# Separate PSUM banks for attention's value products, and one branch's gate blocks placed between the heads' projections

## The chip, the cores and the metric

The kernel runs on one core of a Trainium2 chip. A core has five engines with a queue each: TensorE (PE, matmuls; PEld is its weight load), VectorE (DVE), ScalarE (ACT), GpSimd (POOL) and SyncE (SP, which here issues the weights' transfers). Matmul results go to PSUM, which has eight banks of 128 partitions x 512 float32; VectorE and ScalarE read them from there. The metric is the device time of one execution in microseconds (us); lower is better. Times are the median of several runs, and one more execution is profiled.

## The reference

One layer of a streaming encoder on 512 tokens of width 1024. The change concerns the first sub-layer, four parallel mixers (A to D) that read the same normalized input `h`, and touches the PSUM banks of all later stages.

```python
h = _rms_norm(x, norm_mix_pre[l])
(a_q, a_k, a_v, f_q, f_k, f_v, f_g, c_u, s_x, s_b, s_c) = jnp.split(h @ w_in[l], cuts, axis=-1)
# A: differential attention, 4 heads, chunk-causal: a = softmax(s0) - lam * softmax(s1);  ya = rms_norm(a @ v)
# B: forgetting attention, 8 heads, frame-causal, bias from cumulative log forget gates;  yf = softmax(s + bias) @ v
# C: convolution branch: GLU, causal depthwise conv of width 31, LayerNorm, silu -> yc
# D: short gated convolution: s_b * conv3(s_c * s_x) -> ys
br = jnp.stack([ya, yf, yc, ys], axis=2)
proj = jnp.einsum('bsnc,ncd->bsnd', br, w_branch[l])
gates = jax.nn.sigmoid(h @ w_gate[l] + b_gate[l]).reshape(B, S, N_BRANCH, D)
mixed = jnp.sum(gates * proj, axis=2) @ w_out[l]
x = x + _rms_norm(mixed, norm_mix_post[l])
```

Cross-attention into 256 memory tokens and a gated MLP of width 2816 follow.

## The kernel before

**Arithmetic.** Each float32 operand is split into a high and a low part, and a product is three matmuls (`mm3`, line 185): high x high, high x low, low x high, all issued in line 178. A projection of 128 output channels over 1024 inputs is 8 x 3 = 24 matmuls of 512 columns (`channel_major`, line 191). Transposes are matmuls with an identity (line 182).

**Blocks.** `run_blocks` (line 151) takes jobs from one list, `all_jobs` (line 1268). Most jobs carry a weight block of 512 KB: `load_raw` (line 118) has SP transfer it into `wr` (2 buffers), ACT makes the high part `wh` (line 138) and DVE the low part `wl` (line 139), four buffers each; then the job's body issues its matmuls and the work that reads its PSUM bank. A job that is only a function (`then`, line 894) runs between the bodies.

**Background tasks.** The attention heads, the convolution and the norms are generators in a queue (`Background`, line 44). `bg.tick()` lets up to two of them take steps beside the blocks, by a clock of matmul time and by a cost that each step gives; `bg.drain(name)` runs the tasks of that name to their end.

**Final order.** What is traced is not yet the order on the engines: the framework orders instructions by a timeline of its own, which takes buffers into account, and writes the waits between engines. Each engine then works through its queue in that order.

**PSUM.** `bank(tag)` (line 90) takes one of the eight banks: tag `mm` has four, `sc` (scores) two, `tr` (transposes) two. Before, projections and attention's value products (`values`, line 634) both take `mm`. A value product of a head in A (`a_task`, line 650) takes its bank at step 3 and gives it back after step 5; a task of B (`f_task`, line 793) takes two banks so.

**The order of the mixer** (`mixer_jobs`, line 901): the convolution's input (C), the short convolution (D), D's gates and products, the values of A, then for each of A's four heads its q and k projection (`qk_jobs`, line 591), after which that head's task joins the queue. Then, after `bg.drain("conv")`, the gates of C (`gate_blocks(2, "c")`, line 862): for each of four pairs of output blocks two gate blocks (24 matmuls each, evicted by ACT's tanh in line 871) and one branch block (two products of 12 matmuls, evicted by DVE in line 883 and added in line 884). Then the tasks of A are drained, and the values, q and k of B follow, with A's gates between them.

**A head of A.** `qk_jobs` writes q and k into a tile `qk` (2 buffers; POOL clears two halves of it in line 600) with ACT (lines 604, 612, 613) and DVE (lines 605 and 614, two of each). `a_task` goes through four blocks of 128 queries: scores into two `sc` banks, mask and maximum (DVE, line 671), exponentials (ACT, line 676), the reciprocal and lambda (lines 678, 679), the difference of the two softmaxes (lines 680, 681), a transpose through a `tr` bank, and its split into high and low parts (lines 109, 110), which the value products read. The last steps normalize the head's output (lines 686 to 705).

**Other stages named below.** The bias of B's scores is made on POOL (line 830) and added with the maximum on DVE (line 836). D's B product is read in line 564. The first four up-projections (`up_jobs`, line 1188) are done in two halves of tokens and hold their banks meanwhile; the down-projection (line 1225) uses all eight banks.

Of the kernel before, what the change touches and what calls it, by code (L numbers as in the profile page):

```python
# [16 lines left out]
F32 = mybir.dt.float32  # L17
# [7 lines left out]
P = 128  # L25
# [55 lines left out]
def hybrid_layer(ctx: ExitStack, tc: tile.TileContext, a: dict, out: bass.AP):  # L81
# [5 lines left out]
    psum = ctx.enter_context(tc.tile_pool(name="ps", bufs=4, space=PSUM))  # L87
    dram = ctx.enter_context(tc.tile_pool(name="dr", bufs=1, space=DRAM))

    def bank(tag="mm"):  # L90
        return psum.tile([P, 512], F32, tag=tag, name=f"ps_{tag}", bufs=4 if tag == "mm" else 2)

    x_d, mem_d = a["x"][0], a["mem"][0]
    w_in, w_gate, w_out = a["w_in"][0], a["w_gate"][0], a["w_out"][0]
# [54 lines left out]
    bg = Background(0.7, 2)  # L149
# [140 lines left out]
    for i, plan in enumerate(plans):  # L290
        r_t = m1p.tile([P, P], F32, tag="fbias" if i == 2 else "ck", name=f"rows{i}", bufs=2)
        n = 0
# [10 lines left out]
    for i in range(2):  # L303
        keep(PE.matmul(gain[i], ones, gain_row[:, i * 512:(i + 1) * 512], start=True, stop=True))

    glu = [bank() for _ in range(2)]

    def busy(n):

# [24 lines left out]
    turned = {}  # L334
# [3 lines left out]
        keep(V.scalar_tensor_tensor(y01[t][:, sl], xs[:, t, sl], r01[t], gain[half], ALU.mult, ALU.mult))  # L338

    def turn(t, half):  # L340
        ps = turned[t, half] = bank("mm" if half else "tr")
        for k in range(4):
            keep(PE.transpose(ps[:, k * P:(k + 1) * P], y01[t][:, (half * 4 + k) * P:(half * 4 + k + 1) * P], ident))  # L343

# [43 lines left out]
    w_g = [split_weights(*raw, V, lambda ins: casts.append(keep(ins))) for raw in raw_g]  # L388


    glu.extend(bank() for _ in range(2))
    for i in range(2):
        for p in range(3):
            first_half(i, p, w_g[i], glu[2:])
# [22 lines left out]
    half = {}  # L417
# [232 lines left out]
    def a_task(h, qk, v):  # L650
        es, pt, av = {}, None, None
        for step in range(6):
            if step in (3, 5):
                if av is None:
                    av = bank()
                vh, vl = (x[:, :, h * P:(h + 1) * P] for x in v[0])
                values(av, lambda kt: ((vh[:, kt], 0), (vh[:, kt], 1), (vl[:, kt], 0)), pt, step // 2 - 1)
            cost = 0.0
            if 1 <= step <= 4:
                if step in (1, 3):  # L660
                    pt = pt_tiles()
                to_keys_major(es.pop(step - 1)[:, 0], step, pt[0], pt[1], (step - 1) % 2)
                cost += 0.1 + 0.15 * step
            if step < 4:
                qt, w = step, (step + 1) * P
                e = es[qt] = e4()
                st = m1p.tile([P, 8], F32, tag="st8", name="st8", bufs=4)
                for c in range(2):
                    ps = bank("sc")
                    scores(ps, qk, c, qt * P, w)  # L670
                    V.tensor_tensor_reduce(e[:, c, :w], ps[:, :w], mask_a[:, S - w:], scale=1.0,  # L671
                                           scalar=-3.0e38, op0=ALU.add, op1=ALU.max,
                                           accum_out=st[:, c:c + 1])
                V.tensor_scalar(st[:, 2:4], st[:, 0:2], -HD ** -0.5, None, ALU.mult)
                for c in range(2):
                    A.activation(e[:, c, :w], e[:, c, :w], AF.Exp, bias=st[:, 2 + c:3 + c],
                                 scale=HD ** -0.5, accum_out=st[:, 4 + c:5 + c])
                V.reciprocal(st[:, 6:8], st[:, 4:6])
                V.tensor_scalar(st[:, 7:8], st[:, 7:8], lam, None, ALU.mult)
                A.activation(e[:, 1, :w], e[:, 1, :w], AF.Copy, scale=st[:, 7:8])  # L680
                V.scalar_tensor_tensor(e[:, 0, :w], e[:, 0, :w], st[:, 6:7], e[:, 1, :w], ALU.mult,
                                       ALU.subtract)
                cost += 0.6 + 0.0035 * w
            if step == 5:
                e = e4()
                A.copy(e[:, 0], av)
            yield cost, 3.5

        ps = bank("tr")
        for t in range(NT):  # L690
            transpose(ps[:, t * P:(t + 1) * P], e[:, 0, t * P:(t + 1) * P])
        A.activation(e[:, 1], ps, AF.Square, scale=1.0 / math.sqrt(P))
        ms = m1p.tile([P, NT], F32, tag="ms4", name="ms4", bufs=2)
        V.tensor_reduce(ms, e[:, 1].rearrange("p (t c) -> p t c", t=NT), AX.X, ALU.add)
        r = rstd_of(m1p, [ms], NT)
        V.tensor_tensor(e[:, 0].rearrange("p (t c) -> p t c", t=NT),
                        ps.rearrange("p (t c) -> p t c", t=NT),
                        r.unsqueeze(2).to_broadcast([P, NT, P]), ALU.mult)
        yield 1.5, 3.5
        ps2 = bank("tr")  # L700
        for t in range(NT):
            transpose(ps2[:, t * P:(t + 1) * P], e[:, 0, t * P:(t + 1) * P])
        if "a" not in y:
            y["a"] = (y8(), y8())
        split(ps2, y["a"][0][:, h], y["a"][1][:, h], half["dn"])
        yield 0.6, 0.0
# [5 lines left out]
    def vf_jobs(dst):  # L712

        ps, held = {}, []
        groups = ((0, 256), (256, 520))

        def products(kb, tokens):
            hi, lo = held[kb]
            for t in tokens:
                sl = slice(t * P, (t + 1) * P)  # L720
                for k in range(2):
                    kk = kb * 2 + k
                    for g, (c0, c1) in enumerate(groups):
                        mm3(ps[t, g][:, :c1 - c0], ht[0][:, kk, sl], ht[1][:, kk, sl], hi[:, k, c0:c1],
                            lo[:, k, c0:c1], kk == 0, kk == NK - 1)

        def done(t):
            for g in range(2):
                hs = slice(4 * g, 4 * g + 4)
                split(ps[t, g][:, :256].rearrange("p (h c) -> p h c", h=4), dst[0][:, t, hs, 0], dst[0][:, t, hs, 1])  # L730
            V.tensor_copy(dst[1][:, t], ps[t, 1][:, 256:264])

        for kb in range(4):
            def body(hi, lo, kb=kb):
                held.append((hi, lo))
                if kb == 0:
                    dst.append(m1p.tile([P, NT, 8, 2, HD], F32R, tag="v", name="v"))
                    dst.append(m1p.tile([P, NT, 8], F32, name="fz_raw"))
                    ps.update({(t, g): bank() for t in range(2) for g in range(2)})
                products(kb, (0, 1))  # L740
                if kb < 3:
                    return
                done(0)
                done(1)
                bg.tick()
                ps.update({(t, g): bank() for t in range(2, 4) for g in range(2)})
                for b in range(4):
                    products(b, (2, 3))
                    bg.tick()
                done(2)  # L750
                done(3)
                forget_gates(dst[1])

            yield *cols(w_in, O_FV, BR + 8, kb * 2, 2), body
# [38 lines left out]
    def f_task(p, qk, v):  # L793
# [4 lines left out]
        for j in range(2):  # L798
            t = m1p.tile([P, S], F32, tag="ck", name="ck", bufs=2)
# [3 lines left out]
        es, pts, av = {}, None, None  # L803
        for step in range(6):
            if step in (3, 5):
                if av is None:
                    av = [bank(), bank()]
                for j in range(2):
                    hl = v[0][:, :, 2 * p + j]
                    values(av[j], lambda kt: ((hl[:, kt], 0), (hl[:, kt], 1)), pts[j], step // 2 - 1)  # L810
# [11 lines left out]
            if step < 4:  # L822
# [3 lines left out]
                for j in range(2):  # L826
# [7 lines left out]
                    ps = bank("sc")  # L834
# [59 lines left out]
    def then(f):  # L894

        return None, None, f
# [4 lines left out]
    def mixer_jobs():  # L901
        yield from c_jobs()
        yield then(lambda: bg.add(lam_task(), "lam"))
        yield from d_jobs()
        yield then(lambda: bg.add(conv_norm_task(), "conv"))
        yield from gate_blocks(3, "d")
        yield then(lambda: y.pop("d"))
        yield from v_jobs(O_AV, va)
        for h in range(4):
            yield from qk_jobs(O_AQ, O_AK, h, lambda qk, h=h: bg.add(a_task(h, qk, va), "a"))  # L910
        yield then(lambda: bg.drain("conv"))
        yield from gate_blocks(2, "c")
        yield then(lambda: bg.drain("a"))
        yield from vf_jobs(vf)
        yield from kv_blocks(0)
        ga = gate_blocks(0, "a")
        for p in range(1, 4):
            yield from kv_blocks(p)
            for _ in range(4):
                yield next(ga)  # L920
        yield then(lambda: bg.drain("f"))


    ns = SimpleNamespace()
# [263 lines left out]
    def up_jobs():  # L1188
# [16 lines left out]
        for n in range(2 * NF):  # L1205
            def body(hi, lo, n=n):
                j, i = divmod(n, 2)
                if n > 3:
                    ps = bank()
# [2 lines left out]
                    return  # L1212
                if n == 0:
                    bg.drain("n0")
                ps = bank("mm" if n % 2 else "sc")
                channel_major(ps, (hi, lo), ns.hf, slice(0, S // 2))
                held.append((j, i, ps, (hi, lo)))
                if n == 3:
# [6 lines left out]
    def down_jobs():  # L1225
        tail = 4
        held, ps = [], []
# [5 lines left out]
        for kk in range(NF):  # L1233
            def body(hi, lo, kk=kk):
                if kk == 0:
                    tags = (("mm", "mm"), ("mm", "mm"), ("sc", "sc"), ("tr", "tr"))
                    ps.extend([bank(n) for n in pair] for pair in tags)
                if kk < NF - tail:
                    for t in range(NT):
# [6 lines left out]
                for t in range(NT):  # L1246
# [11 lines left out]
                    for i in range(2):  # L1258
                        sl = slice(i * 512, (i + 1) * 512)
                        parts = 2 if (t, i) == (NT - 1, 1) else 1  # L1260
                        for q in range(parts):
                            n = 512 // parts
# [50 lines left out]
```

## Time and profile before

| | |
|---|---|
| median of 3 runs | 1109.14 us (1108.85 to 1110.48) |
| profiled execution | 1108.61 us, of which its span (first to last instruction) 1106.8 us |
| granted clock of TensorE, mean | 0.998 |
| matmul and weight-load records | 5445 each |
| DMA issues on SP | 207, most of them weight blocks of 512 KB |
| weight cast, ACT line 138 | 180 x 1.05 us |
| weight split, DVE line 139 | 180 x 1.23 us |
| projection matmul, 512 columns, line 178 | record of 0.38 to 0.40 us |
| q eviction, DVE line 605; k eviction, DVE line 614 | 16 x 0.69 us each |
| gate eviction, ACT line 871 | 0.69 us |
| branch eviction, DVE line 883; sum, line 884 | 24 x 0.69 us each |

The stages by time: C's and D's input to about 127 us, D's gates to 195, A's values to 219, A's q and k to 277, C's gates to 363, B's values to 386, B's q and k with A's gates to 524, B's gates to 597, output projection to 640, cross-attention to 731, the MLP to the end.

How the profile is read: a share of busy time is an average over these stages. [...] In the chain of waits, the work that ended last is followed back through whatever released it; pieces of another engine in it are times when PE's next matmul hung on that engine. In the timeline, a bracket after an instruction gives the idle time of its engine just before it and what ended it.

### The profile page before, as it was taken

What the parts mean: (1) busy time and instruction counts of PE and PEld (TensorE: products, weight loads), DVE (VectorE), ACT (ScalarE), POOL (GpSimd) and SP (SyncE); (2) the same over time, 40 slices, a digit from 0 to 9 for tenths busy, and PEclk for the clock granted to TensorE, in tenths of its full rate; (3) what the DMA queues carried; (4) which work ended last, traced back from release to release, by engine and by line L of the source; (5) the groups of instructions that cost most, each with busy time, mean ns of one, the idle gap of its engine ahead of it and who ended that gap; (6) DMA issues with size and microseconds to landing.
All of it is one profiled execution on the core that took longest, in us unless ns stands there. A gap on an engine that the chain in (4) does not pass through costs nothing.

```text
span 1106.8 us, 14168 instructions
## 1 busy us (share of the span) xinstructions
PE 1091.0 (99%) x5445; PEld 913.1 (82%) x5445; DVE 693.9 (63%) x1128; ACT 464.9 (42%) x783; POOL 97.9 (9%) x186
## 2 busy tenths in 40 slices
PE   8999999999999999999999999999999999999997
PEld 7888888887878988888888899788888888888886
DVE  5899985457665367857464477677666666642224
ACT  5322222467564255554443365455444444431111
POOL 3000001000101013323010110120000000000001
PEclk9999999999999999999999999999999999999999
DMA  6433432332212243233262253233333333322222
GB/s 197 115 95 94 102 94 81 92 96 58 77 58 78 77 120 104 82 96 107 65 209 96 76 174 115 73 96 115 95 95 95 96 95 95 96 96 95 95 76 76
DMA packets 145849, 109.29 MB, mean 99 GB/s; under 512 B 3648, under 2 KB 133293, under 8 KB 145782
## 3 DMA queue, kind: packets, MB, share of 16 engines
q1 hardware_dynamic: 143221, 99.85, 29.9%
q0 software_dynamic: 2560, 8.54, 2.8%
q8 instruction: 43, 0.70, 0.3%
q14 instruction: 25, 0.20, 0.1%
HBM read 106.27 MB, written 2.11 MB: 98 GB/s over the span
## 4 chain that ended last, share of the span: by engine, by line
PE 94%; DVE 2%; DMA 1%; issue 1%; ACT 1%; POOL 0%; POOLq 0%; DVEq 0%; SPq 0%; ACTq 0%
PE ps_mm L178 80%; PE ps_sc L178 7%; PE ps_tr L182 3%; PE ps_tr L178 3%; PE ps_mm L359 1%; DVE wl L139 1%; DMA wr<-in_w_xo 1%; DMA wr<-in_w_xkv 0%; ACT wh L138 0%; DMA xs<-in_x 0%; POOL st_r L208 0%; DVE e L671 0%; PE ps_tr L343 0%; PE ps_mm L343 0%; ACT hth L109 0%
## 5 line engine op out<-in xcount | busy, mean ns | idle before, releaser
L139 DVE TENSOR_TENSOR wl<-wr,wh 128x1024 fp32r<-128x1024 f32 (+1 forms) x180 | 221.4, 1231 | 221.6 <-ACT wh L138 220.9
L178 PE MATMUL ps_mm<-htl,wh 128*128 128x512 f32 (+1 forms) x944 | 359.9, 381 | 0.0
L178 PE MATMUL ps_mm<-hth,wh 128*128 128x512 f32 (+1 forms) x944 | 359.8, 381 | 0.0
L178 PE MATMUL ps_mm<-hth,wl 128*128 128x512 f32 (+1 forms) x944 | 358.7, 380 | 0.0
L138 ACT CAST wh<-wr 128x1024 fp32r<-128x1024 f32 (+1 forms) x180 | 188.6, 1050 | 349.1 <-PE ps_mm L178 223.0
L178 PEld LDWEIGHTS ps_mm<-hth,wl 128*128 128x128 f32 x944 | 177.4, 188 | 34.5
L178 PEld LDWEIGHTS ps_mm<-hth,wh 128*128 128x128 f32 x944 | 177.6, 188 | 33.9
L178 PEld LDWEIGHTS ps_mm<-htl,wh 128*128 128x128 f32 x944 | 177.6, 188 | 33.0
L507 DVE SCALAR_TENSOR_TENSOR y<-y,par,y 128x499 f32<-128x499 f32 (+28 forms) x120 | 82.7, 729 | 0.2
L178 PE MATMUL ps_mm<-y,wh 128*128 128x512 f32 x256 | 81.2, 395 | 0.0
L441 DVE SCALAR_TENSOR_TENSOR c<-ps_mm,par,c 128x510 f32<-128x510 f32 x84 | 62.6, 746 | 1.4
L178 PEld LDWEIGHTS ps_mm<-y,wh 128*128 128x128 f32 x256 | 47.4, 188 | 10.1
L178 PE MATMUL ps_mm<-y,wl 128*128 128x512 f32 x128 | 50.6, 395 | 0.0
L205 POOL TENSOR_SCALAR st_m<-pm,pm 128x1 f32<-128x1 f32 x12 | 4.6, 387 | 480.6 <-ACT junk L1254 357.0
L109 ACT CAST acth<-c 128x512 fp32r<-128x512 f32 x22 | 13.7, 621 | 55.2 <-DVE c L1201 55.2
L109 ACT CAST pth<-ps_tr 128x512 fp32r<-128x512 f32 (+3 forms) x56 | 23.7, 451 | 27.8 <-PE ps_tr L182 24.9
L178 PE MATMUL ps_mm<-wh,actl 128*128 128x512 f32 x88 | 34.7, 394 | 0.0
L178 PE MATMUL ps_mm<-wl,acth 128*128 128x512 f32 x88 | 34.6, 393 | 0.0
L178 PE MATMUL ps_mm<-wh,acth 128*128 128x512 f32 x88 | 34.4, 394 | 0.0
L110 DVE TENSOR_TENSOR ptl<-ps_tr,pth 128x512 fp32r<-128x512 f32 (+3 forms) x56 | 27.8, 512 | 9.5 <-ACT pth L109 9.1
L1195 ACT ACTIVATE c<-ps_mm,par 128x512 f32<-128x512 f32 x42 | 32.5, 773 | 0.0
L830 POOL TENSOR_SCALAR fbias<-ck,cq 128x128 f32<-128x128 f32 (+3 forms) x32 | 25.5, 805 | 70.6 <-DVE st L836 66.9
(294 smaller groups left out, 1620.3 us busy)
## 6 DMA issues: line engine op xcount, KB each, us to landing
wr<-in_w_up SPq DMA_DIRECT2D x44, 512.0 KB
wr<-in_w_in SPq DMA_DIRECT2D x38, 512.0 KB
wr<-in_w_gate SPq DMA_DIRECT2D x32, 512.0 KB
wr<-in_w_down SPq DMA_DIRECT2D x22, 512.0 KB
wr<-in_w_branch SPq DMA_DIRECT2D x16, 512.0 KB
wr<-in_w_out SPq DMA_DIRECT2D x8, 512.0 KB
wr<-in_w_xkv SPq DMA_DIRECT2D x8, 512.0 KB
wr<-in_w_in SPq DMA_DIRECT2D x4, 520.0 KB
```

The source lines that it names most:

```text
L109: A.copy(hi, ps)
L110: V.tensor_tensor(lo, ps, hi.bitcast(F32), ALU.subtract)
L138: order(A.copy(hi[:, :n], raw[:, :n]))
L139: low.tensor_tensor(lo[:, :n], raw[:, :n], hi[:, :n].bitcast(F32), ALU.subtract)
L178: PE.matmul(ps, lhs, rhs, start=start, stop=stop)
L182: PE.transpose(ps, x, ident[:n, :n])
L205: G.tensor_scalar(m, parts[0], parts[1], EPS, ALU.add, ALU.add)
L359: keep(PE.matmul(banks[c][:, :S // 2], w[p == 1][:, k, c * P:(c + 1) * P], ht[p == 2][:, i * 4 + k, :S // 2], start=(i, p, k) == (0, 0, 0) ...
L441: V.scalar_tensor_tensor(dst[:, s:], src[:, :S - s], w(k), dst[:, s:], ALU.mult, ALU.add)
L507: V.scalar_tensor_tensor(dst[:, s:], src[:, :S - s], pc("conv_dw", k * 4 + j), dst[:, s:], ALU.mult, ALU.add)
L830: G.tensor_scalar(bias[:, :w], ck[j][:, :w], -1.0, cq[:, qt, head:head + 1], ALU.mult, ALU.add)
L1195: A.activation(c[:, i], ps, AF.Identity, bias=pc("fb", ch), scale=pc("fdw2", ch))
```

## The change

- `bank` gets a fourth tag `av`, and all four tags have two banks. A call without a tag takes `av` and `mm` in turn (`av` first) while `turn_of.shared` is set, otherwise `mm` alone. `share(False)` stands as a job ahead of A's heads, `share(True)` behind B's last task; the latter also resets the turn.
- The value products of A and B take `av`. Where four banks are taken at once (the values of B, the down-projection, the start), two are `mm` and two `av`.
- C's twelve gate and branch blocks are dealt out: none after head 0's q and k, two after head 1's, four after head 2's, six after head 3's, each time after `bg.drain("conv")`.
- The first four up-projections take `mm` and `sc` in the other order.

```diff
--- before.py
+++ after.py
@@ -87,8 +87,18 @@
     psum = ctx.enter_context(tc.tile_pool(name="ps", bufs=4, space=PSUM))
     dram = ctx.enter_context(tc.tile_pool(name="dr", bufs=1, space=DRAM))
 
-    def bank(tag="mm"):
-        return psum.tile([P, 512], F32, tag=tag, name=f"ps_{tag}", bufs=4 if tag == "mm" else 2)
+
+
+    turn_of = SimpleNamespace(n=0, shared=True)
+
+    def bank(tag=None):
+        if tag is None:
+            turn_of.n += 1
+            tag = "av" if turn_of.shared and turn_of.n % 2 else "mm"
+        return psum.tile([P, 512], F32, tag=tag, name=f"ps_{tag}", bufs=2)
+
+    def share(shared):
+        return None, None, lambda: vars(turn_of).update(n=1, shared=shared)
 
     x_d, mem_d = a["x"][0], a["mem"][0]
     w_in, w_gate, w_out = a["w_in"][0], a["w_gate"][0], a["w_out"][0]
@@ -303,7 +313,7 @@
     for i in range(2):
         keep(PE.matmul(gain[i], ones, gain_row[:, i * 512:(i + 1) * 512], start=True, stop=True))
 
-    glu = [bank() for _ in range(2)]
+    glu = [bank("mm") for _ in range(2)]
 
     def busy(n):
 
@@ -338,7 +348,7 @@
         keep(V.scalar_tensor_tensor(y01[t][:, sl], xs[:, t, sl], r01[t], gain[half], ALU.mult, ALU.mult))
 
     def turn(t, half):
-        ps = turned[t, half] = bank("mm" if half else "tr")
+        ps = turned[t, half] = bank("av" if half else "tr")
         for k in range(4):
             keep(PE.transpose(ps[:, k * P:(k + 1) * P], y01[t][:, (half * 4 + k) * P:(half * 4 + k + 1) * P], ident))
 
@@ -388,7 +398,7 @@
     w_g = [split_weights(*raw, V, lambda ins: casts.append(keep(ins))) for raw in raw_g]
 
 
-    glu.extend(bank() for _ in range(2))
+    glu.extend(bank("av") for _ in range(2))
     for i in range(2):
         for p in range(3):
             first_half(i, p, w_g[i], glu[2:])
@@ -652,7 +662,7 @@
         for step in range(6):
             if step in (3, 5):
                 if av is None:
-                    av = bank()
+                    av = bank("av")
                 vh, vl = (x[:, :, h * P:(h + 1) * P] for x in v[0])
                 values(av, lambda kt: ((vh[:, kt], 0), (vh[:, kt], 1), (vl[:, kt], 0)), pt, step // 2 - 1)
             cost = 0.0
@@ -736,14 +746,14 @@
                 if kb == 0:
                     dst.append(m1p.tile([P, NT, 8, 2, HD], F32R, tag="v", name="v"))
                     dst.append(m1p.tile([P, NT, 8], F32, name="fz_raw"))
-                    ps.update({(t, g): bank() for t in range(2) for g in range(2)})
+                    ps.update({(t, g): bank(("mm", "av")[g]) for t in range(2) for g in range(2)})
                 products(kb, (0, 1))
                 if kb < 3:
                     return
                 done(0)
                 done(1)
                 bg.tick()
-                ps.update({(t, g): bank() for t in range(2, 4) for g in range(2)})
+                ps.update({(t, g): bank(("mm", "av")[g]) for t in range(2, 4) for g in range(2)})
                 for b in range(4):
                     products(b, (2, 3))
                     bg.tick()
@@ -804,7 +814,7 @@
         for step in range(6):
             if step in (3, 5):
                 if av is None:
-                    av = [bank(), bank()]
+                    av = [bank("av"), bank("av")]
                 for j in range(2):
                     hl = v[0][:, :, 2 * p + j]
                     values(av[j], lambda kt: ((hl[:, kt], 0), (hl[:, kt], 1)), pts[j], step // 2 - 1)
@@ -906,10 +916,14 @@
         yield from gate_blocks(3, "d")
         yield then(lambda: y.pop("d"))
         yield from v_jobs(O_AV, va)
-        for h in range(4):
+        yield share(False)
+        gc = gate_blocks(2, "c")
+        for h, n in enumerate((0, 2, 4, 6)):
             yield from qk_jobs(O_AQ, O_AK, h, lambda qk, h=h: bg.add(a_task(h, qk, va), "a"))
-        yield then(lambda: bg.drain("conv"))
-        yield from gate_blocks(2, "c")
+            if n:
+                yield then(lambda: bg.drain("conv"))
+            for _ in range(n):
+                yield next(gc)
         yield then(lambda: bg.drain("a"))
         yield from vf_jobs(vf)
         yield from kv_blocks(0)
@@ -919,6 +933,7 @@
             for _ in range(4):
                 yield next(ga)
         yield then(lambda: bg.drain("f"))
+        yield share(True)
 
 
     ns = SimpleNamespace()
@@ -1212,7 +1227,7 @@
                     return
                 if n == 0:
                     bg.drain("n0")
-                ps = bank("mm" if n % 2 else "sc")
+                ps = bank(("mm", "sc")[n % 2])
                 channel_major(ps, (hi, lo), ns.hf, slice(0, S // 2))
                 held.append((j, i, ps, (hi, lo)))
                 if n == 3:
@@ -1233,7 +1248,7 @@
         for kk in range(NF):
             def body(hi, lo, kk=kk):
                 if kk == 0:
-                    tags = (("mm", "mm"), ("mm", "mm"), ("sc", "sc"), ("tr", "tr"))
+                    tags = (("mm", "mm"), ("av", "av"), ("sc", "sc"), ("tr", "tr"))
                     ps.extend([bank(n) for n in pair] for pair in tags)
                 if kk < NF - tail:
                     for t in range(NT):
```

## The prediction

> **What bounds the kernel now.** I read the page's busy shares first, then the stretches of 25 us, then the chain of waits inside the worst stretches, then the timeline there.
>
> ```profile
> PE 1091.0 (99%) x5445; PEld 913.1 (82%) x5445; DVE 693.9 (63%) x1128; ACT 464.9 (42%) x783; POOL 97.9 (9%) x186
> ...
> PE   8999999999999999999999999999999999999997
> ...
> PEclk9999999999999999999999999999999999999999
> ```
>
> The tensor engine (PE) is busy 99% of 1106.8 us at the full clock, so a change can win only what PE still loses between matmuls. The matmuls before and after are the same 5440; none is removed.
>
> ```profile
> core 0: us, PE busy (x) PEld busy (x) DVE busy (x) ACT busy (x) POOL busy (x), PEclk, DMA share, GB/s
> 225.00:250.00 25.00, 24.57 (x113) 19.92 (x111) 14.73 (x32) 14.76 (x28) 0.00 (x0) 1.00 0.30 85
> 250.00:275.00 25.00, 22.80 (x113) 18.30 (x114) 18.98 (x57) 18.39 (x44) 2.08 (x4) 1.00 0.22 64
> 275.00:300.00 25.00, 25.00 (x134) 21.10 (x132) 14.01 (x29) 13.40 (x24) 1.28 (x2) 1.00 0.21 64
> 300.00:325.00 25.00, 24.19 (x120) 19.46 (x119) 19.14 (x57) 15.13 (x37) 2.68 (x4) 1.00 0.22 64
> 50.00:75.00 25.00, 25.00 (x110) 20.38 (x109) 24.71 (x36) 6.79 (x9) 0.00 (x0) 1.00 0.31 85
> ```
>
> Three of these stretches, all in differential attention (237 to 350 us), are not full: 0.43, 2.20 and 0.81 us idle. That is a lower bound: a 512-column matmul's record lasts 0.39 us, but the next one starts 0.228 us after it (25 us / 110 in the dense stretch 50:75), so an idle gap hides under the tail of a record. By start times, against 0.228 us (512 columns), 0.116 (256) and 0.109 (a transpose), PE lost 2.36 us at 248.1 to 252.7, 1.27 at 267.7 to 269.4, 1.15 at 305.6 to 308.2 and 0.44 at 322: **5.2 us**. Outside attention it lost 8 us in the first 25 us and about 5 between 640 and 750, which this change does not address. The chain of waits names what PE waits for:
>
> ```profile
> 247.94 0.36 PE ps_sc L178 x2
> ...
> 248.89 0.47 DVE e L671
> 249.36 0.01 DVE st L671
> 249.37 1.14 DVE wl L139
> 250.50 0.41 DVE e L681
> 250.91 0.04 issue
> 250.96 0.44 PE ps_tr L182 x2
> ```
>
> Scores, their softmax on VectorE, and the transposes of the result follow one another with no projection in between: the path leaves PE for 2.6 us, and a 1.2 us weight split (L139) sits in the middle. Why no projection stood there:
>
> ```profile
> 247.55 0.39 PE L178 MATMUL ps_mm<-hth,wl 128*128 128x512 f32 x1
> ...
> 252.44 1.09 POOL L600 MEMSET qk<- 64x512 f32 x2 [31.87 <-PE ps_sc L178]
> ...
> 256.92 0.69 DVE L605 TENSOR_TENSOR qk<-ps_mm,qk 64x512 fp32r<-64x512 f32 x1
> ```
>
> Head 2's q projection ends at 247.94, but its qk tile (two buffers) is free only when head 0's last scores are done (the memset at 252.44), so its bank is read out at 257.61, 9.7 us later. The same count gives 7.5 us for head 3's q. Projections run into the heads they should cover.
>
> **The change, part by part.** *Gates dealt between q and k.* Twelve blocks (eight gate, four branch) move from behind head 3 to behind heads 1, 2 and 3 (2, 4, 6). Each carries its SP transfer (512 KB), an ACT cast (1.05 us), a DVE split (1.23), 24 matmuls (5.5 us) and its eviction (0.69 on ACT or DVE; a branch block has two L883 and two L884 of 0.69). Their number is unchanged; only the order on all queues is. Head 2's q now comes two gate blocks later, 11 us, and by then head 0 is past its scores: the cluster at 248 gets 24 gate matmuls between scores and transposes. In the changed PE order I counted the matmuls between each head's score group and the transposes that need it: 34 to 60 issues, 7 to 12 us, against a softmax step that in the rows takes 4.3 us (256 columns: two L671 of 0.42, two L676 of 0.5 + 0.19, L680 0.5, L681 0.48, small ones 0.9) to 6 us (512), plus up to 2.5 us for a weight split and an eviction ahead in DVE's queue. All fit. So I take off the whole 5.2 us; at least the 3.4 us of plain idle, at most 6.4 us (the excess by start times in all five stretches, 7.9, less the 0.3 that each dense stretch has too).
>
> *The weights' transfers* on SP's queue follow the new order. In this stage a split weight is ready 15 us before its first use (cast at 218.6, used at 235.8), and DMA runs at 0.2 to 0.3 share: cost 0. Past 15 us of delay it would be paid in full.
>
> *Two banks for projections, two for value products.* Until the queue leaves the mixer, projections rotate through two banks, where four were shared with the value products. A bank must be read within the next job. Gate blocks are: 1.45 us from last matmul to the end of L871, against 5.5 us (gate) or 2.7 us (half a branch). q and k are not: 4.2 to 9.7 us (below). I walked the new order by these times. One wait shows: head 2's k is evicted in two halves on DVE, and in the new DVE order the second half (L614) stands behind the first branch product (L883), which waits for PE. Only seven transposes (0.76 us) part that product's last matmul from head 2's first scores, which need the L614: 0.18 + 0.69 + 0.69 - 0.76 = 0.8 us, and 1.9 us if DVE comes there about 1 us late, as my walk has it. I take **1.3 us**. Behind the L614 on DVE are only later softmax steps.
>
> *The same in forgetting attention.* Gate 0 there needs the bank of pair 1's q. That bank is read by 409.33 (L605 at 408.64, behind a bias step that waits for POOL), and PE would ask at about 409.1: **0.3 us**, 0 to 0.9. *Leaving the mixer*, banks alternate again; the second gate of the last branch is put behind pair 3's value products and asks for their bank some 0.3 us before it is read (541.45): **0.2 us**, 0 to 0.5.
>
> *Elsewhere* banks alternate strictly, which needs every bank back after four jobs as before. In the short-convolution stage the B product's bank is held up to 15.1 us (L564), longer than two jobs (11 us), but it is one of a tag's two, and the other is read in 0.8 to 1.4 us; the new order swaps two pairs of jobs there. Their weights have the same 15 us in hand. Cost 0; if a tag's two banks were ever both held, 15.1 - 11 = 4 us each time. The first up-projections swap tags: the third asks at 731.9 for a bank read by 731.79, so 0.
>
> **Sum:** -5.2 + 1.3 + 0.3 + 0.2 = -3.4 us. The profiled execution took 1108.61 us (span 1106.8 and 1.8 around it), 0.5 below the median of 1109.14, so its span should become 1103.4 and the median **1105.7 us**.
>
> [...]
>
> **The rivals.** (1) *Everything is won:* no new wait, small gaps gone too: -6.4, **1102.7 us**. For it: the new order was made with the two banks known. Against: the 1.3 us above.
>
> (2) *The stalls move.* At 305.6 and 322 PE lost 1.6 us in two heads although gate blocks (from 277.2 on) stood all around: there the scores of three groups were queued at once behind two score banks. If each of the four heads loses 0.8 us so, 3.2 of the 5.2 stay, and with the 1.8 of new waits it is -0.2: **1108.9 us**. Against: the new order has fewer such bunches.
>
> (3) *Two banks are too few (slower).* If nothing but the next projection covers a q or k eviction, PE waits for the eviction's time beyond 5.5 us: 9.7 and 7.5 us (q of heads 2 and 3), 6.3 and 6.2 (q and k of pair 1), 5.95 (k of pair 2) give 4.2 + 2.0 + 0.8 + 0.7 + 0.45 = 8.1 us. With the 5.2 won, +2.9: **1112.0 us**. It makes the kernel slower from 7.4 us of such waits on. For it: these rows. Against: the two longest came from the qk tile that the new order frees in time, and behind most q and k jobs stand scores and value products as well.
>
> **How the numbers follow.** A measurement of this kernel tells 0.2%, 2.2 us, from nothing. My sum with its bounds (a gain of 2.2 to 5 us) gets 0.58, (1) 0.08, (2) 0.20, (3) 0.14. So faster 0.66, same 0.20, slower 0.14. The forecast's own range is 1104.1 to 1106.9; with (1) nearly whole and most of (2), 1102.8 to 1109.6 holds 8 in 10.
>
> **What would show it.** Right: PE busy in the stretches between 225 and 325 us at 25.00; the chain there with no VectorE piece over 0.5 us; head 2's q read out in under 7 us; a wait of about 1 us of PE for L614 near 276 us, between the first branch product and head 2's first scores; the stages before 219 us and after 570 us as long as now. Wrong: gaps ahead of a projection's first matmul, with the release by L605 or L614 (rival 3); VectorE pieces at the score groups as large as now (rival 2); a stage without attention that changes by over 1 us, which I have at nothing.

## The result, and the profile after

| | before | after |
|---|---|---|
| median | 1109.22 us (4 runs, 1108.85 to 1110.48) | 1103.39 us (4 runs, 1103.28 to 1103.45) |
| profiled execution / its span | 1108.61 / 1106.8 us | 1103.45 / 1101.7 us |

The ratio is 0.9945 (95% interval 0.9933 to 0.9956): 5.8 us by the medians, 5.1 us by the two spans. The forecast was 1105.7 us, so the gain came out 2.4 us larger (5.8 against 3.4): the median lies 0.7 us below the forecast's own range (1104.1 to 1106.9) and inside the wider one (1102.8 to 1109.6). One execution among the experiments below, the first with the banks alone, took 4079.8 us at a mean granted clock of 1.0; it is left out, and that kernel was profiled again.

The busy shares of the page after, and below them the stretches of 25 us (after the stretch's bounds come its length and the busy time of PE, PEld, DVE, ACT and POOL with their instructions, then granted clock, DMA share and GB/s):

```profile
PE 1088.4 (99%) x5445; PEld 912.7 (83%) x5445; DVE 695.2 (63%) x1128; ACT 463.4 (42%) x783; POOL 100.6 (9%) x186
```

```profile
225.00:250.00 25.00, 25.00 (x118) 20.66 (x117) 16.20 (x39) 14.97 (x31) 0.00 (x0) 1.00 0.29 85
250.00:275.00 25.00, 25.00 (x130) 21.04 (x130) 17.20 (x48) 17.34 (x41) 2.08 (x4) 1.00 0.29 85
275.00:300.00 25.00, 25.00 (x130) 20.93 (x129) 15.76 (x35) 12.64 (x27) 2.94 (x4) 1.00 0.22 64
300.00:325.00 25.00, 25.00 (x125) 20.91 (x124) 17.21 (x41) 14.94 (x32) 1.04 (x2) 1.00 0.29 85
```

The three stretches that were not full (24.57, 22.80, 24.19) are full. By start times, as in the prediction, the five stretches from 225 to 350 us had 7.93 us of excess before and have 1.88 now, 0.3 to 0.5 in each, which every dense stretch has. So 6.05 us were won there; the 0.9 us that is missing from the spans' 5.1 was lost in small pieces elsewhere, most of it between 640 and 750 us (about 1 us more excess than before, mostly in stalls that were there before too).

The chain of waits after, in the same stretch as the lines shown of before:

```profile
248.37 0.40 PE ps_sc L188 x4
248.77 4.65 PE ps_mm L188 x20
253.42 0.93 PE ps_sc L188 x4
254.35 1.38 PE ps_mm L188 x6
255.72 0.12 PE ps_av L188
...
272.34 2.81 PE ps_mm L188 x12
275.15 0.76 PE ps_tr L192 x7
275.92 0.29 PE ps_sc L188 x3
276.20 5.57 PE ps_mm L188 x24
281.77 0.06 PE ps_sc L188
```

Every piece is PE's: behind each score group stands a projection, and the softmax on VectorE no longer shows.

### The profile page after: what moved, and what is told of

Same layout as the page of the kernel before. It is cut to its first block, busy times and chain, and to the rows that moved or that the text cites. A ratio compares the mean times of both kernels' runs of the same rounds, so it can differ in the third digit from the quotient of the medians.

```text
span 1101.7 us, 14173 instructions
## 1 busy us (share of the span) xinstructions
PE 1088.4 (99%) x5445; PEld 912.7 (83%) x5445; DVE 695.2 (63%) x1128; ACT 463.4 (42%) x783; POOL 100.6 (9%) x186
## 4 chain that ended last, share of the span: by engine, by line
PE 94%; DMA 2%; DVE 1%; ACT 1%; issue 1%; POOL 0%; POOLq 0%; DVEq 0%; SPq 0%; ACTq 0%
PE ps_mm L188 49%; PE ps_av L188 30%; PE ps_sc L188 8%; PE ps_tr L192 3%; PE ps_tr L188 3%; DVE wl L149 1%; DMA wr<-in_w_xo 1%; ACT wh L148 1%; PE ps_mm L369 1%; PE ps_av L369 1%; DMA wr<-in_w_xkv 0%; DMA wr<-in_w_xq 0%; DMA xs<-in_x 0%; POOL st_r L218 0%; ACT hth L119 0%
## 5 line engine op out<-in xcount | busy, mean ns | idle before, releaser
L149 DVE TENSOR_TENSOR wl<-wr,wh 128x1024 fp32r<-128x1024 f32 (+1 forms) x180 | 222.1, 1235 | 216.0 <-ACT wh L148 215.3
L188 PE MATMUL ps_mm<-hth,wh 128*128 128x512 f32 (+1 forms) x608 | 233.7, 385 | 0.4 <-ACT hth L119 0.2
L188 PE MATMUL ps_mm<-hth,wl 128*128 128x512 f32 (+1 forms) x608 | 232.5, 382 | 0.0
L188 PE MATMUL ps_mm<-htl,wh 128*128 128x512 f32 (+1 forms) x608 | 232.3, 382 | 0.2 <-DVE htl L120 0.2
L188 PEld LDWEIGHTS ps_mm<-hth,wh 128*128 128x128 f32 x608 | 114.4, 188 | 22.2 <-ACT hth L119 0.5
L188 PE MATMUL ps_av<-hth,wh 128*128 128x512 f32 (+1 forms) x336 | 127.2, 379 | 0.2
L188 PE MATMUL ps_av<-htl,wh 128*128 128x512 f32 (+1 forms) x336 | 126.9, 378 | 0.0
L188 PE MATMUL ps_av<-hth,wl 128*128 128x512 f32 (+1 forms) x336 | 126.9, 378 | 0.0
L188 PEld LDWEIGHTS ps_av<-hth,wh 128*128 128x128 f32 x336 | 63.2, 188 | 13.1 <-DVE e L864 0.5
L188 PEld LDWEIGHTS ps_av<-hth,wl 128*128 128x128 f32 x336 | 63.2, 188 | 12.6
L188 PEld LDWEIGHTS ps_av<-htl,wh 128*128 128x128 f32 x336 | 63.2, 188 | 12.4
```

The source lines that it names most:

```text
L149: low.tensor_tensor(lo[:, :n], raw[:, :n], hi[:, :n].bitcast(F32), ALU.subtract)
L188: PE.matmul(ps, lhs, rhs, start=start, stop=stop)
```

## The experiments

Each median stands beside runs of the kernel before on the same chip (1108.8 to 1108.9 us; 1109.2 for the changed kernel), and the ratio is taken against those.

| kernel | median, us | ratio (95%) | excess of 225:250, 250:275, 300:325, 325:350 |
|---|---|---|---|
| before | 1109.2 | 1 | 2.2, 2.8, 2.4, 0.4 |
| after | 1103.39 | 0.9945 (0.9933 to 0.9956) | 0.4, 0.4, 0.3, 0.3 |
| banks alone | 1105.36 | 0.9964 (0.9951 to 0.9978) | 0.4, 2.5, 0.4, 0.3 |
| dealing alone | 1107.1 | 0.9979 (0.9970 to 0.9988) | 2.0, 3.1, 0.3, 0.7 |
| dealing 0, 0, 6, 6 | 1105.21 | 0.9969 (0.9956 to 0.9981) | 0.4, 2.5, 0.4, 0.3 |
| dealing 0, 2, 0, 10 | 1102.90 | 0.9944 (0.9931 to 0.9956) | 0.4, 0.4, 0.4, 0.4 |
| dealing 0, 1, 0, 11 | 1103.14 | 0.9948 (0.9935 to 0.9962) | 0.4, 0.4, 0.4, 0.4 |
| later value product, before's banks and order | 1104.64 | 0.9964 (0.9951 to 0.9976) | 0.3, 3.3, 0.6, 0.3 |
| later value product, dealt, before's banks | 1107.93 | 0.9990 (0.9982 to 0.9999) | 0.3, 2.5, 2.5, 1.7 |
| three banks and one, dealt | 1106.52 | 0.9977 (0.9967 to 0.9986) | 0.3, 0.4, 0.3, 0.5 |
| three banks and one, not dealt | 1111.94 | 1.0023 (1.0014 to 1.0032) | 0.3, 5.0, 0.4, 0.3 |

The last column is the start-time excess in us, of which 0.3 to 0.4 is nothing. It comes from one profiled execution each. In two of these the granted clock fell to 0.50 for about 3.4 us (it is 0.93 on the mean of 250:275 in both; in the dealing alone 0.50 in 253:254 and 0.60 in 254:257): some 1.7 of the 3.1 us of the dealing alone, and some 1.4 of the 5.0 us of three and one not dealt, are matmuls at half the clock and not stalls.

**The two halves of the change, each alone.** The banks alone, on the changed kernel:

```diff
-        gc = gate_blocks(2, "c")
-        for h, n in enumerate((0, 2, 4, 6)):
+        for h in range(4):
             yield from qk_jobs(O_AQ, O_AK, h, lambda qk, h=h: bg.add(a_task(h, qk, va), "a"))
-            if n:
-                yield then(lambda: bg.drain("conv"))
-            for _ in range(n):
-                yield next(gc)
+        yield then(lambda: bg.drain("conv"))
+        yield from gate_blocks(2, "c")
```

> All bank edits of the change, but C's twelve gate and branch blocks stay together behind head 3, as in the kernel before. Theory 1 (the gain is the dealing: gate matmuls between a head's scores and its transposes): nothing is won, 1109.2 us or up to 4 us more, since head 2's q then still waits 9.7 us for its qk tile with only two banks to rotate; PE still idles in the stretches 250 to 275 and 300 to 325. Theory 2 (the gain is the value products' own banks, which no longer keep one of four banks from the projections): at least half of the 5.8 us is won, 1106.3 us or less, and the stretch 250 to 275 is full.

The dealing alone is the reverse edit on the kernel before:

> The kernel before with only the dealing of C's blocks (0, 2, 4, 6 behind the heads); projections and value products share four banks as before. Theory 1 (dealing): the whole gain, 1103.4 us within 1 us, PE at 25.00 from 225 to 325 us. Theory 2 (banks): under half of the gain, 1106.3 us or more. A third possibility, that neither does it alone: both this run and the one with the banks alone stay within 1.5 us of 1109.2.

My theory of that time, which is the prediction's, fails in both. The banks alone win 3.5 us, the dealing alone 1.7 by the medians. With the dealing alone the cluster at 248 to 253 us, for which I had credited it with 24 gate matmuls, stayed, although two gate blocks now stood behind head 1. The three later clusters went: from 264 to 275 us the excess is 0.2 us (1.9 before), from 300 to 325 us 0.3 (2.4 before).

The median of 1107.1 us hides this, because the clock fell in most executions. Of the eleven, seven have a mean granted clock of 0.996 or 0.997 and took 1106.9 to 1108.5 us; four have 0.999 and took 1105.1 to 1105.3, which is 3.4 us less than the two executions of before in the same session with 0.999 (1108.6 us). So without a fall of the clock the dealing alone wins about as much as the banks alone, and the two gains do not add up to more than 5.8 us because both edits take away the three later clusters.

**How the blocks are dealt**, with the new banks: two other tuples in the `enumerate` line.

> The changed kernel with the dealing 0, 0, 6, 6: no block between head 1's k and head 2's q. If the cluster of 2.4 us near 248 us came from head 2's q asking for its qk tile too early, it returns here and the other clusters stay away: 1103.4 + 2.4 = 1105.8 us, and up to 4 us more if the two banks then stop PE as well (q's eviction lagged 9.7 us, against 5.5 for the next projection). If any dealing gives the cover, 1103.4 us within 0.7.

> The changed kernel with the dealing 0, 2, 0, 10: two blocks ahead of head 2, none between heads 2 and 3. If the clusters near 305 and 322 us (1.15 and 0.44 us) came from heads 2 and 3 running side by side, they return and the two ahead of them stay away: 1103.4 + 1.6 = 1105.0 us. If two blocks ahead of head 2 are all that matters, 1103.4 us within 0.7.

The first gave 1105.21 us: 1.96 us of stall came back, but at 257 to 260 us and with a wait for a bank at its end, which is the second half of what was expected there and not the first. The second was expected at 1105.0 and gave 1102.90: nothing need stand between heads 2 and 3, and the clusters at 305 and 322 us did not come from these two heads running side by side.

**What the clusters have in common.** I went back to the trace of before, to the first matmuls of the value products (PE's timeline; `pth` is the transposed softmax, `hth,wh` the first matmul of a projection):

```profile
252.68 0.50 PE L178 MATMUL ps_sc<-qk 128*128 128x256 f32 x2 [0.30 <-DVE st L671]
253.01 0.28 PE L178 MATMUL ps_mm<-pth,v 128*128 128x256 f32 x1
253.13 0.40 PE L178 MATMUL ps_mm<-hth,wh 128*128 128x512 f32 x1
...
270.60 0.56 PE L178 MATMUL ps_mm<-pth,v 128*128 128x128 f32 x2
271.00 0.40 PE L178 MATMUL ps_mm<-hth,wh 128*128 128x512 f32 x1
...
307.02 1.11 PE L178 MATMUL ps_sc<-qk 128*128 128x512 f32 x4 [0.64 <-DVE st L671]
308.18 0.39 PE L178 MATMUL ps_mm<-pth,v 128*128 128x256 f32 x1
308.40 0.39 PE L178 MATMUL ps_mm<-hth,wh 128*128 128x512 f32 x1
...
323.06 0.39 PE L178 MATMUL ps_mm<-pth,v 128*128 128x256 f32 x2
323.29 0.39 PE L178 MATMUL ps_mm<-hth,wh 128*128 128x512 f32 x1
```

Behind each cluster stands the first matmul of a head's value product (at 253.01, 270.77, 308.18 and 323.17 us; in the second case the rest of the head before comes in between, and the second and fourth are merged into the row that starts just before them), and a projection follows at once: 0.12, 0.23, 0.22 and 0.12 us later for the four heads. By the bank numbers in the built program, that projection's bank had been read at 240.69, 265.08, 295.33 and 318.97 us, 12.4, 5.9, 13.1 and 4.3 us earlier, so a free bank is not what it lacked. It stands in PE's queue behind the value product, which waits for the softmax of its own head. That is theory 3, *order of taking*: tiles of one tag get their banks in the order in which the list of jobs asks, and PE's queue is laid out so; a value product that asks early and starts late holds back the next projection. The rule is inferred from the order seen here. In the changed kernel, the same two on PE's timeline:

```profile
248.13 0.64 PE L188 MATMUL ps_sc<-qk 128*128 128x128 f32 x4
248.60 0.45 PE L188 MATMUL ps_mm<-hth,wh 128*128 128x512 f32 x1
...
255.56 0.28 PE L188 MATMUL ps_av<-pth,v 128*128 128x256 f32 x1
```

Head 0's value product starts at 255.56, and the block behind it in the list at 248.60, 7 us ahead of it.

**Theory 3 put to the test.** First the banks alone again, for a profile:

> The same kernel as with the banks alone, for a profile of an undisturbed execution. New theory 3 (order of taking): in the kernel before, the projection that follows a value product in the list of jobs took its bank only 0.12 to 0.23 us after that value product had taken its own (253.01 and 253.13; 270.77 and 271.00 us), though its bank had been free for 12 us; banks of one tag are handed out in the order of the list, so a value product that waits for its softmax holds back every projection behind it. With a tag of their own the value products hold back nobody: head 2's k starts before head 0's value product, the two clusters at 248 and 268 us shrink to under 1.5 us together, and what is left of the 5.2 us is one wait of about 2 us for the two banks (head 2's q is read late, as with the dealing 0, 0, 6, 6). If theory 1 holds (the qk tile alone), the cluster at 248 us is there as before, about 2.4 us.

Its stretches (columns as above):

```profile
250.00:275.00 25.00, 23.37 (x122) 19.39 (x121) 18.20 (x46) 18.34 (x43) 2.08 (x4) 1.00 0.23 64
275.00:300.00 25.00, 25.00 (x131) 21.01 (x130) 16.03 (x37) 13.34 (x28) 2.64 (x4) 1.00 0.26 75
300.00:325.00 25.00, 25.00 (x124) 20.83 (x123) 17.83 (x51) 15.38 (x35) 1.78 (x3) 1.00 0.25 73
```

As expected: the four clusters are gone, and one stall of 1.96 us is left, 1.10 us of it ahead of head 1's scores and 0.86 ahead of the next projection (PE's timeline):

```profile
258.28 0.97 PE L188 MATMUL ps_sc<-qk 128*128 128x384 f32 x4 [0.94 <-DVE st L681]
259.95 0.50 PE L188 MATMUL ps_mm<-hth,wh 128*128 128x512 f32 x1 [0.69 <-DVE qk L615]
```

Its chain of waits:

```profile
253.92 0.48 PE ps_sc L188 x2
...
255.77 0.70 DVE qk L615
...
256.66 1.23 DVE wl L149
...
259.20 0.70 DVE qk L615
259.90 0.04 issue
259.95 5.86 PE ps_mm L188 x24
```

The two L615 read head 2's q, which ended at 248.66; its bank is free at 259.89, 11.2 us later. First its `qk` tile is in use until head 0's last scores (POOL clears it from 254.91); then the second read stands in VectorE's queue behind a weight split (L149), head 1's maximum and half of head 2's k. With two banks the next projection but one, head 3's q, starts 0.06 us after that. This is rival 3's wait, at the place that it named (4.2 us there, 1.96 measured). What the dealing adds to the banks is to take it away:

> The changed kernel with the dealing 0, 1, 0, 11: one gate block (24 matmuls, 5.5 us) between head 1's k and head 2's q instead of two or none. With none, TensorE lost 1.96 us at 258 to 260 us, waiting for head 2's q to be read out of one of two banks, and the median was 1105.2 to 1105.4 us; with two it lost nothing. If q's wait for its qk tile is what decides, 5.5 us of work more than cover 1.96 us: 1103.2 us within 0.8. If it is the whole two-block order that matters, 1104.5 us or more.

One gate block ahead of head 2 is enough (1103.14 us, no stall over 0.15 us from 25 to 530 us), as expected.

Then the value product's place in the list, without any bank of its own, in the kernel before:

```diff
-        es, pt, av = {}, None, None
+        es, pt, av, pts = {}, None, None, []
...
-            if step in (3, 5):
+            if step in (4, 5):
                 if av is None:
                     av = bank()
                 vh, vl = (x[:, :, h * P:(h + 1) * P] for x in v[0])
-                values(av, lambda kt: ((vh[:, kt], 0), (vh[:, kt], 1), (vl[:, kt], 0)), pt, step // 2 - 1)
+                values(av, lambda kt: ((vh[:, kt], 0), (vh[:, kt], 1), (vl[:, kt], 0)), pts[step - 4], step - 4)
...
                     pt = pt_tiles()
+                    pts.append(pt)
```

> The kernel before (four shared banks, C's blocks behind head 3) with one edit in a head of A: the first value product is issued, and takes its bank, at step 4 of the head and not at step 3, so that in the list of jobs it stands behind one more projection. Theory 3 (order of taking): in the changed order on TensorE head 2's k now comes before head 0's value product, so the cluster of 2.4 us near 248 us goes, and with four banks head 2's q may be read late without a wait: most of the 5.2 us is won, 1104.0 to 1106.0 us. If the value products need banks of their own, nothing is won: 1108.5 us or more.

1104.64 us: an edit that gives the value products no bank of their own wins 4.2 us by the medians, and by the ratios as much as the banks alone (0.9964 both). The cluster at 248 is down to 0.34 us (at 254). Of the 3.3 us left in the next stretch, 2.4 lie at 270 to 275 us. There a value product waits for its softmax (0.99 us for ACT's line 109 is the longest piece), and nothing covers it, because the banks are short for once: q and k of head 3 and the two value products hold all four, and the next gate block starts at 275.08, after a bank is read at 275.02.

> The same edit on top of the dealing 0, 2, 4, 6, with four shared banks. Theory 3: the dealing alone kept only the stall at 248 to 253 us, which this edit takes away: 1103.4 us within 1, what the changed kernel reaches with its own banks. If banks of their own are needed: 1107 us, as with the dealing alone.

This expectation failed: 1107.93 us, 4.5 more than I wrote. The edit moved the value products in the list, and the stalls went with them (PE's timeline):

```profile
308.16 0.71 PE L178 MATMUL ps_sc<-qk 128*128 128x512 f32 x2
310.70 0.39 PE L178 MATMUL ps_mm<-pth,v 128*128 128x256 f32 x1 [1.83 <-ACT pth L109]
310.93 0.39 PE L178 MATMUL ps_mm<-hth,wh 128*128 128x512 f32 x1
...
346.43 0.39 PE L178 MATMUL ps_mm<-pth,v 128*128 128x256 f32 x1 [1.11 <-ACT pth L109]
346.65 0.40 PE L178 MATMUL ps_mm<-hth,wh 128*128 128x512 f32 x1
```

PE stands 2.0 and 1.3 us before two value products, 0.7 and 0.9 us at two more, and each time a projection starts within 0.25 us of the value product. So it is in 15 of the 16 heads of the four kernels with one shared tag (before, dealing alone, and both with the later value product); the 16th is the one at 275 us that lacked a bank. Where the value product falls against the softmax decides whether this costs nothing or 2.4 us. My mistake was to expect one order to be good everywhere; the mechanism is borne out.

**Two and two banks, or three and one.** Three banks for projections, one for A's value products (in B the second of a pair takes one of the three):

```diff
-            tag = "av" if turn_of.shared and turn_of.n % 2 else "mm"
-        return psum.tile([P, 512], F32, tag=tag, name=f"ps_{tag}", bufs=2)
+            tag = "av" if turn_of.shared and turn_of.n % 4 == 1 else "mm"
+        return psum.tile([P, 512], F32, tag=tag, name=f"ps_{tag}", bufs={"mm": 3, "av": 1}.get(tag, 2))
...
-                    ps.update({(t, g): bank(("mm", "av")[g]) for t in range(2) for g in range(2)})
+                    ps.update({(t, g): bank("av" if t + g == 0 else "mm") for t in range(2) for g in range(2)})
...
-                    av = [bank("av"), bank("av")]
+                    av = [bank("av"), bank("mm")]
...
```

> The changed kernel with three banks for projections and one for A's value products. Theory 3: as the changed kernel, 1103.4 us within 1, a little more if head 1's value product now waits for head 0's bank (in the changed kernel it starts 1.5 us before that bank is read). If two banks for the value products are needed, 1105.5 us or more.

> Order of jobs as in the kernel before (C's blocks behind head 3); of the four banks three are for projections and one is for A's value products alone (in B the second of a pair of value products takes one of the three). Theory 3 (order of taking): a gain like that of two and two banks, 1105.3 us within 1.2, although projections have three banks: what counts is that the value products have their own tag. If the number of banks counted (two each are what it takes), 1107.5 us or more.

Dealt, A's heads are as full as in the changed kernel (last column), so the number of banks on either side does not matter there. The 3.1 us by which this kernel is slower than the changed one lie behind them: 2.3 us at 382 us, in the values of B, where I had to spread a claim of four banks over the tags in another way, and 0.8 at 364. The stall at 382 us is a wait for a weight transfer (4.39 us of DMA in the chain, from 376.57 us, and 1.05 us of ACT's cast behind it) that the page had not shown before; what it hangs on I did not pursue. Not dealt, the forecast missed by 6.6 us: the same stall (2.5 us at 387) and 4.5 us at 263 to 270, of which some 3 are stall and some 1.4 the half clock (granted 0.50 from 266.3 to 269.7 us; four score matmuls from 266.88 take 1.86 us in the chain of waits, where four of 512 columns take 0.93 at 253.42 in the changed kernel). Part of the miss is the clock: three of the eleven executions have a mean granted clock of 0.999 and took 1109.1 to 1109.7 us, still 3.8 us or more above the forecast; eight have 0.994 to 0.997 and took 1110.6 to 1114.0. With three banks the planner ran q and k of head 2 and q of head 3 ahead; all three waited for a `qk` tile, and their banks were read to the end at 268.03, 269.88 and 278.71 us. The next projection starts at 268.54. Here a bank more did not help against a tile that is late; more work piled up behind it.

**The dealing alone once more**, since its times scatter:

> The kernel with the dealing alone once more: its times lay between 1105.1 and 1108.5 us, and its profiled execution of 1108.4 us shows the granted clock at 0.50 to 0.60 between 253 and 257 us, after 5 us in which TensorE was half idle. If the clock is what parts its runs, a run near 1105 to 1106 us has 1.00 there and the same stalls at 248 to 253 us; a run near 1108 us has the low clock again. Theory 3 wants in both that the gate block behind head 0's value product starts right after it (253.60 and 253.81 us).

Its stretches of 2 and 3 us around the stall (columns as above, the granted clock being the third from the end):

```profile
246.00:249.00 3.00, 2.29 (x12) 1.60 (x11) 2.33 (x7) 2.44 (x6) 0.00 (x0) 1.00 0.10 29
249.00:251.00 2.00, 1.50 (x5) 1.08 (x6) 1.50 (x10) 1.44 (x5) 0.00 (x0) 0.75 0.15 37
251.00:253.00 2.00, 1.21 (x6) 0.81 (x5) 1.44 (x7) 1.00 (x5) 1.04 (x2) 0.50 0.78 225
253.00:255.00 2.00, 2.00 (x7) 1.61 (x7) 1.26 (x6) 1.84 (x4) 0.00 (x0) 0.50 0.00 0
255.00:257.00 2.00, 2.00 (x7) 1.57 (x6) 1.15 (x4) 1.20 (x4) 0.00 (x0) 0.54 0.00 0
257.00:259.00 2.00, 2.00 (x10) 1.64 (x9) 0.24 (x1) 0.00 (x0) 0.00 (x0) 1.00 0.00 0
```

The granted clock was 0.50 from about 250 to 257 us here, and the value product and its projection stood as theory 3 wants (252.97, 253.19). This execution took 1107.09 us with a mean granted clock of 0.996. The four of 1105.1 to 1105.3 us have 0.999, so no such fall can have been in them: 6.8 us at half the clock take 0.003 off the mean. No profile of one of them was kept, so their stalls were not seen.

No version beats the changed kernel by more than can be told: 1102.90 and 1103.14 us against 1103.39.

## Why the prediction was right or wrong

**Sign and stage: right. Size: near, in part by luck.** PE is full where it was to become full, and 6.05 us were won in these stretches, inside the bounds given (3.4 to 6.4) and above the 5.2 that I took. The whole gain was forecast too small (3.4 against 5.8 us), mainly because 1.6 of the 1.8 us of new waits did not appear. That the 5.2 us came out near is luck: I put all of them down to the dealing, which alone clears 2.9 of them.

**The cause: wrong.** The step that failed reads "Why no projection stood there": I held head 2's q, waiting for its `qk` tile, to be why PE had nothing to do. The late q is real, but before had two more projections to run and free banks for them. What kept them was the value product ahead of them under the same tag. So the part that I costed as a pure loss, "two banks for projections, two for value products", takes away all four clusters by itself, while the dealing, to which I gave the 5.2 us, takes away three of them (2.9 us) and leaves the one of 2.4 us that I had explained. Through which waits the dealing clears the other three was not followed up. In the sum none of this showed, since both edits were made together.

**The dealing** is worth 2.0 us beside the banks (1105.36 to 1103.39, from two sessions; the stall in the trace is 1.96): it takes away rival 3's wait, which I had costed at nothing because the dealing was there. Of the two, either would have been forecast wrongly alone.

**The 1.3 us for head 2's k: mis-sized, 0.** VectorE's order was as predicted (its timeline in the changed kernel):

```profile
273.17 0.68 DVE L624 TENSOR_TENSOR qk<-ps_mm,qk 64x512 fp32r<-64x512 f32 x1
...
275.19 0.69 DVE L893 SCALAR_TENSOR_TENSOR ge<-ge,ps_mm 128x512 f32<-128x512 f32 x1 [1.27 <-PE ps_mm L188]
275.91 0.69 DVE L624 TENSOR_TENSOR qk<-ps_mm,qk 64x512 fp32r<-64x512 f32 x1
```

(lines 614 and 883 of before). The second half is ready only at 276.60, after PE's turn for the scores at 275.92. But three of the four score matmuls need only the first half, and the fourth, which needs the second, stands 24 projection matmuls later in PE's queue, at 281.77 in the chain shown above. I had taken the score group for one piece.

**Forgetting attention's 0.3: did not appear** (no stall over 0.14 us from 375 to 525 us). **Leaving the mixer's 0.2: right**, 0.22 us at 534.5 us, ahead of the second gate.

**Rivals.** (1) comes closest: the real 1103.39 lies 0.7 above its 1102.7. (2) did not happen. (3) is a real wait of this kernel, but only where nothing is dealt ahead of head 2. Head 2's q was read out 5.3 us after its end, under the 7 that I named. **The weights' transfers** cost nothing in A, as put, and outside A and B no stage changed by over 1 us (the most, by excess, is some 0.8 us in cross-attention).

Fewer banks for the projections do cost something where q is late: head 2's q shows it (1.96 us with the banks alone), but the larger effect was that groups which are *not* alike shared one rotation (the clusters of 5.2 us).

## What to carry to other kernels

When a tensor engine is idle although banks are free, look at which instruction stands first in its queue and which tiles asked for a bank ahead of the one that could run: tiles that start late and tiles that can start at once should not draw from one rotation (with the banks alone this was worth 3.5 us). In the seven kernels here in which the value products had a tag of their own, no stall of this kind was left in A; moving their request in the list helped in one order and not in the other (1104.64 and 1107.93 us). And look at the clock of each execution: the dealing alone won 1.7 us by its median and 3.4 where the clock held. And run each half of a two-part change alone before believing which half pays.

## What the runs showed of the hardware

In the profiles the granted clock fell while TensorE was partly busy. In the second profile of the dealing alone it fell to 0.50 at about 250 us, when PE had been busy 2.29 of the 3 us up to 249, and stayed there until about 257, although PE was busy all the time from 253; a 512-column matmul then started every 0.43 us, where the dense stretches have 0.228. In the first profile of this kernel it fell at 253 us, when PE had been busy 2.24 of the 4 us before (249 to 253). That alone does not bring it about: the profile of before shows the clock at 1.00 in the same place and up to 265 us, with PE busy 2.56 of the same 4 us and a stall of the same size (2.4 us), and three and one dealt kept 1.00 from 375 to 400 us, where PE was idle for 2.15 us. What decides is open.

The kernels with a stall of over 1 us in A or in B's values scatter by 1.2 to 4.9 us (before 1107.7 to 1110.6, dealing alone 1105.1 to 1108.5, three and one not dealt 1109.1 to 1114.0), the three without by 0.2 to 0.9. In two of them the mean granted clock parts the executions without overlap, as given above: dealing alone (0.999 up to 1105.3 us, 0.997 or less from 1106.9) and three and one not dealt (0.999 up to 1109.7, 0.997 or less from 1110.6). In the kernel before it does not (0.999 from 1108.5 to 1110.4, 0.997 from 1107.8 to 1110.6), so the scatter there has another cause, which was not found.
